# A list scheduler's table: measured durations, and one port shared by GpSimd and VectorE

## The chip, the cores and the metric

The kernel runs on one core of one Trainium2 chip. The metric is the device time of one execution in microseconds (us), the median of several runs. A core has five instruction streams that run side by side and meet only at semaphores: PE (TensorE, matrix products), DVE (VectorE), ACT (ScalarE), POOL (GpSimd) and SP (SyncE, which here issues nearly all DMA transfers). Each stream runs in program order: an instruction that waits holds up all that stands behind it on its engine.

## The reference

One decoder block over 16 meta tokens and 1024 tokens of width 1024, in float32. It has a differential-attention branch (a) and a gated-linear-attention branch (b, GLA below), whose gated sum goes through a last projection and a norm.

```
u = rms_norm(h, norm_w);  proj = u @ w_in          (1040 x 1024 @ 1024 x 9232)
a_q, a_k, a_v, a_z, g_q, g_k, g_v, g_z, g_lr, gate_a, gate_b = split(proj)
(branch a: 8 heads, partial rope on q and k, two causal softmaxes per head)
p = softmax(q1 k1) - lam * softmax(q2 k2)
y_a = (rms_norm(p @ v) * silu(a_z)) @ w_branch_a
(branch b: 4 heads of width 128, values of width 256)
b = cumsum(log_sigmoid(g_lr @ gate_w2 + gate_b) / 16)
a[t, j] = sum_c q[t, c] k[j, c] exp(b[t, c] - b[j, c])   for j <= t
o = a @ v + (q exp(b)) @ state;  state = exp(b_last) state + (k exp(b_last - b))' v
y_b = (rms_norm(o) * silu(g_z)) @ w_branch_b
out = rms_norm(h + (sigmoid(gate_a) y_a + sigmoid(gate_b) y_b) @ w_out)[16:]
```

## The kernel before, in words

Products in float32 are made of three products of halves (high x high, high x low, low x high), so that most groups of PE instructions come in threes. The program has four parts, one behind the other.

1. The first norm, the transposes of x and the four g_k projections (0 to 79.8 us).
2. Most of the input projections, as Strassen products in a fixed order (79.8 to 594 us).
3. The GLA stage (594 to 891 us): four heads, each in two halves of 512 tokens. Among the work of the heads lie *fillers*: projections that later stages need (`Jobs.cols` L410 to L412 and `Jobs.rows` L431 to L438, results in tiles `ps_proj`), with `rope(0, ...)` for the attention's rotated queries.
4. Attention over eight heads, with the projection of branch b between, then that of branch a, then the output projection and the last norm (891 to 1399 us).

Parts 1, 3 and 4 are not written in program order. Each operation is entered in a list (`Schedule.op`) with its engine, an estimated duration, what it depends on, the buffer ring from which it takes a slot and a priority. `Schedule.run` then plays the list through once, when the program is built: it keeps a time for each engine, starts the operation that can start earliest, and within 0.05 us of a tie the one with the better priority. Each engine's program order is the order of these planned starts; the durations in the list have no other effect. Part 2 does not pass through it.

A half of a GLA head goes through seven *levels* (L1437 to L1482): POOL makes four differences of the cumulated decay (L1398, tile `xl`), ACT takes their exponential (L1441), DVE multiplies them by k and q (L1405), PE makes the *level product* (L1412, tile `ps_l`), and DVE picks the part of it that counts (L1416). There are two buffers each for `xl` and `ps_l`. Behind the levels come the diagonal (L1422), the output (L1488, L1489), the state (L1476, L1482), a norm (L1504), the transposes (L1509) and the split and store of the result (L1514 to L1525). POOL does the last step of that split (L1521) and SP stores it to `d_ob`.

When the last GLA operation and its store are done, a step in SP's list (`change`) closes the stage's buffers. Attention takes their place: POOL clears the tiles `vm` (L1593), and the loads of values and later keys follow (`early`).

Of the kernel before, what the change touches and what calls it, by code (L numbers as in the profile page):

```python
# [67 lines left out]

class Schedule:
# [9 lines left out]
    def op(self, eng, us, run, deps=(), take="", use=(), prio=0.0, lat=None):  # L79
        o = Op(eng=eng, us=us, run=run, deps=deps, take=take, use=use, prio=prio)  # L80
# [10 lines left out]
    def run(self):  # L91
        now = dict.fromkeys(("PE", "ACT", "DVE", "POOL", "SP"), 0.0)
        ready = {e: [] for e in now}
# [27 lines left out]
        while len(order) < len(self.ops):  # L121
            best = None
            for e in now:
                pick = None
                for o in ready[e]:
                    r = at(o)
                    if r is not None:
                        r = max(r, now[e])
                        if pick is None or r < pick[0] - AHEAD:
                            pick = (r, o)  # L130
# [4 lines left out]
            now[o.eng] = o.end  # L135
            if o.take:
# [12 lines left out]
def tile_hybrid_block(  # L149
# [191 lines left out]
    class Jobs:  # L341
# [7 lines left out]
        def weights(self, src, us_lo=0.6, eng="DVE", scale=None, where=None, ring="w", pre=None):  # L349
# [31 lines left out]
            for c in range(2):  # L381
                a = op("ACT", 0.52, lambda c=c: hi(c), (ld,) + tuple(w["ops"]), take="" if c else ring,
                       use=(("raw", ld),), prio=PR["W"])
                b = op(eng, us_lo, lambda c=c: lo(c), (a,), use=(("raw", ld),), prio=PR["W"])
# [14 lines left out]
        def cols(self, ws, pieces, evac):  # L399
            prev = None  # L400
            for t0, n in pieces:
                for i, w in enumerate(ws):
                    b = {}

                    def run(kc, b=b, w=w, t0=t0, n=n):
# [9 lines left out]
                        [lambda k=k, run=run: run(k) for k in range(KC)], n / 512 * 0.64,  # L415
# [4 lines left out]
        def rows(self, src, evac, pre=None):  # L420
# [221 lines left out]
    with ExitStack() as es:  # L642
# [15 lines left out]
        def x_tile(i):  # L658
# [28 lines left out]
            r = op("POOL", 0.3, root, (m,), prio=-1)  # L687
            d = op("DVE", SCU, scale, (r,), use=(("xt", ld),), prio=-1)
# [167 lines left out]
        W = [jobs.weights(c[0], 1.2, "POOL") if i < 2 else jobs.weights(c[0]) for i, c in enumerate(cols)]  # L856
# [18 lines left out]
        def sums(k):  # L875
            ts, x = {}, {}
            for i in range(1, 5):
# [16 lines left out]
                t = ts[i] = op("DVE", 0.6, run, (R[r], R["t", 1, k]) + tuple(readers.get(r, ())), prio=30 + k,  # L894
# [4 lines left out]
            for i in range(1, 5):  # L899
# [13 lines left out]
                b = op("DVE", 0.6, lo, (a,) + free("l") + last.get((i, 1), ()), prio=30 + k, use=use)  # L913
# [142 lines left out]
    with ExitStack() as es:  # L1056
# [110 lines left out]
        def rope(base, dst, pieces, lo_t, pre=(None, None)):  # L1167
# [18 lines left out]
            def turns(a, t0, n):  # L1186
# [8 lines left out]
                for q, f in ((0, ALU.subtract), (1, ALU.add)):  # L1195
# [12 lines left out]
                    for s in range(3):  # L1208
                        prev = (op("DVE", n / 960 + 0.07, lambda s=s, turn=turn: turn(s), prev,
# [29 lines left out]
        def gla_head(h):  # L1239
# [10 lines left out]
            for t0, n in KP:  # L1250
# [11 lines left out]
                def low(v=v, c=c, first=t0 == 0):  # L1262
# [11 lines left out]
                    g("DVE", 0.43, lambda v=v, c=c: tt(d["lg"][:, c], d["lg"][:, c], v["t"], ALU.subtract), (m, l),  # L1274
# [4 lines left out]
            for i, (t0, n) in enumerate([(0, NM)] + [(NM + P * i, P) for i in range(8)]):  # L1279
# [3 lines left out]
                if i == 0 or i % 2:  # L1283
# [4 lines left out]
                    scans.append(g("DVE", 0.2, scan, deps, use=(lgu,)))  # L1288
                else:
# [9 lines left out]
                    s = g("DVE", 0.2, scan, deps, take="scn", use=(lgu,))  # L1299
                    scans.append(g("DVE", 0.26, rest, (s,), use=(("scn", s), lgu)))  # L1300
# [32 lines left out]
            def half_ops(hf, st):  # L1333
# [1191 lines left out]
```

## Time and profile before

| | us |
|---|---|
| median of 3 runs | 1395.36 (1394.68 to 1396.65) |
| the profiled execution, its own time | 1400.65 |
| its span, first to last instruction | 1398.9 |
| mean granted TensorE clock | 0.990 |

The trace is of one execution, 5.3 us longer than the median of the runs; 1.75 us of it lie outside the span. Times in the text are from the start of that span. The names of tiles are the program's, with the line that issued the instruction.

### The profile page before, as it was taken

Reading aid. Unit: us, or ns where it says so; the run is one execution under the profiler, and the core shown is the slowest. Engines: PE = TensorE matmul, PEld = TensorE weight load, DVE = VectorE, ACT = ScalarE, POOL = GpSimd, SP = SyncE. Lnnn points to the kernel's source line nnn. Section 1 sums busy time; section 2 is a strip of 40 time slices with the busy share of each in tenths; the row PEclk is TensorE's granted clock in tenths of the full one; section 3 lists DMA queues with packets and bytes.
Section 4 is the critical chain, followed back from the end, with each engine's and each line's share of the span. In section 5 each row is a group of like instructions: output and inputs, shape, how many; then the busy total and the mean of one; then the engine's idle time right before and its main releaser. Section 6 shows DMA issues by size and latency. Waiting matters only on the chain.

```text
span 1398.9 us, 22432 instructions
## 1 busy us (share of the span) xinstructions
PE 1337.4 (96%) x7736; PEld 1158.8 (83%) x7736; DVE 908.3 (65%) x1613; ACT 741.1 (53%) x1608; POOL 626.1 (45%) x731
## 2 busy tenths in 40 slices
PE   6999999999999999988998989999999999999998
PEld 6988889899888888787888979878888888887786
DVE  4745463545555444478888887568777777657775
ACT  7543232653665666554544544568677777522343
POOL 3112232442544233236566475347576665535434
PEclk9999999999999999999999999999999999999999
DMA  6216473324333323385531465769765564678332
GB/s 222 90 67 200 141 231 122 106 84 145 113 113 114 120 99 105 116 287 150 178 119 64 150 205 167 246 201 292 275 224 171 194 208 140 241 271 278 109 119 84
DMA packets 126337, 229.50 MB, mean 164 GB/s; under 512 B 13568, under 2 KB 51648, under 8 KB 126224
## 3 DMA queue, kind: packets, MB, share of 16 engines
q1 hardware_dynamic: 125936, 227.03, 49.2%
q8 instruction: 61, 1.00, 0.3%
q0 software_dynamic: 288, 1.05, 0.3%
q14 instruction: 52, 0.43, 0.1%
HBM read 143.81 MB, written 84.21 MB: 163 GB/s over the span
## 4 chain that ended last, share of the span: by engine, by line
PE 67%; DVE 13%; DMA 5%; issue 5%; POOL 5%; ACT 4%; SPq 1%; POOLq 0%; DVEq 0%; ACTq 0%
PE ps_st L547 28%; PE ps_st L572 6%; DVE xl L1405 3%; PE ps_t L2321 2%; PE ps_s L1698 2%; PE ps_proj L410 2%; PE ps_proj L412 2%; PE ps_proj L411 2%; PE ps_l L1412 2%; PE ps_s L1699 1%; PE ps_y L2321 1%; PE ps_s L2321 1%; PE ps_t L1812 1%; PE ps_y L1981 1%; PE ps_y L1983 1%
## 5 line engine op out<-in xcount | busy, mean ns | idle before, releaser
L495 POOL TENSOR_TENSOR s<-w_raw 128x512 f32<-128x512 f32 x48 | 70.2, 1481 | 199.5 <-DMA w_raw<-in_w_col_dram 146.4
L547 PE MATMUL ps_st<-th,wh 128*128 128x512 f32 x352 | 137.3, 390 | 0.2 <-DVE u L561 0.2
L547 PE MATMUL ps_st<-tl,wh 128*128 128x512 f32 x352 | 137.1, 389 | 0.0
L547 PE MATMUL ps_st<-th,wl 128*128 128x512 f32 x352 | 136.9, 389 | 0.0
L1398 POOL TENSOR_TENSOR xl<-lg 128x128 f32<-128x128 f32 x224 | 108.8, 513 | 60.1 <-PE ps_l L1412 21.2
L230 DVE TENSOR_TENSOR wl<-s,wh 128x512 fp32r<-128x512 f32 x96 | 76.1, 792 | 63.6 <-ACT wh L229 63.5
L229 ACT CAST wh<-s 128x512 fp32r<-128x512 f32 x96 | 59.3, 618 | 105.6 <-PE ps_st L547 51.5
L1727 DVE TENSOR_REDUCE nm<-ps_s 128x1 f32<-128x272 f32 (+7 forms) x128 | 96.5, 765 | 18.9 <-PE ps_s L1701 18.0
L410 PE MATMUL ps_proj<-u_hi,w_hi 128*128 128x346 f32 (+3 forms) x320 | 105.1, 329 | 3.2 <-DVE cc L561 1.7
L1739 ACT ACTIVATE p<-ps_s,nm 128x272 f32<-128x272 f32 (+7 forms) x128 | 96.5, 756 | 19.2 <-DVE nm L1727 13.3
L547 PE MATMUL ps_st<-u_hi,wh 128*128 128x512 f32 x264 | 104.2, 395 | 1.0 <-issue 1.0
L547 PE MATMUL ps_st<-u_lo,wh 128*128 128x512 f32 x264 | 105.0, 398 | 0.0
L547 PE MATMUL ps_st<-u_hi,wl 128*128 128x512 f32 x264 | 103.8, 393 | 0.0
L411 PE MATMUL ps_proj<-u_lo,w_hi 128*128 128x346 f32 (+3 forms) x320 | 99.0, 309 | 0.1
L412 PE MATMUL ps_proj<-u_hi,w_lo 128*128 128x346 f32 (+3 forms) x320 | 98.3, 307 | 0.0
L229 ACT CAST wh<-w_raw 128x512 fp32r<-128x512 f32 x70 | 43.2, 617 | 95.4 <-PE ps_st L547 87.8
L230 DVE TENSOR_TENSOR wl<-w_raw,wh 128x512 fp32r<-128x512 f32 x70 | 59.8, 854 | 49.7 <-ACT wh L229 49.7
L1751 POOL TENSOR_SCALAR p<-p,r,nlam 128x144 f32<-128x144 f32 (+3 forms) x64 | 56.4, 882 | 56.2 <-DVE r L1747 42.8
L495 POOL TENSOR_TENSOR s<-w_raw,s 128x512 f32<-128x512 f32 x22 | 28.4, 1293 | 114.1 <-DVE wl L230 114.1
L547 PEld LDWEIGHTS ps_st<-th,wh 128*128 128x128 f32 x352 | 66.1, 188 | 14.8 <-ACT sg L273 0.6
L547 PEld LDWEIGHTS ps_st<-th,wl 128*128 128x128 f32 x352 | 66.1, 188 | 14.0
L547 PEld LDWEIGHTS ps_st<-tl,wh 128*128 128x128 f32 x352 | 66.1, 188 | 13.8
(402 smaller groups left out, 4390.2 us busy)
## 6 DMA issues: line engine op xcount, KB each, us to landing
w_raw<-in_w_col_dram SPq DMA_DIRECT2D x54, 512.0 KB, 3.6
q<-d_q SPq DMA_DIRECT2D x32, 512.0 KB, 5.1
kk<-d_k SPq DMA_DIRECT2D x16, 520.0 KB, 6.0
d_g<-sg SPq DMA_DIRECT2D x32, 256.0 KB, 2.0
va<-d_v SPq DMA_DIRECT2D x16, 512.0 KB, 5.2
d_q<-qhi SPq DMA_DIRECT2D x24, 256.0 KB, 3.1
d_q<-qlo SPq DMA_DIRECT2D x24, 256.0 KB, 3.6
w_raw<-in_w_row_dram SPq DMA_DIRECT2D x12, 512.0 KB, 3.6
```

Source lines behind the costliest of these rows:

```text
L229: nc.scalar.copy(hi, raw)
L230: (eng or nc.vector).tensor_tensor(lo, raw, hi.bitcast(F32), ALU.subtract)
L410: mm(b["ps"], wh, rh, start=kc == 0, stop=False)
L411: mm(b["ps"], wh, rl, start=False, stop=False)
L412: mm(b["ps"], wl, rh, start=False, stop=kc == KC - 1)
L495: nc.gpsimd.tensor_tensor(r, x, y, op)
L547: mm(ps, w[:, k], x[k], start=start and k == 0 and i == 0, stop=k == KC // 2 - 1 and i == 2, skip_group_check=not start,)
L572: mm(ps[ti // 2][:, r], x[k][:, c], w[:, k % 2], start=start and k == i == 0 and ti % 2 == 0, stop=k == KC // 2 - 1 and i == 2 and ti % 2 ...
L1398: nc.gpsimd.tensor_tensor(dst, x if e else ref, ref if e else x, ALU.subtract)
L1727: nc.vector.tensor_reduce(b, ps, AX.XY if len(ps.shape) == 3 else AX.X, ALU.max, negate=True)
L1739: act(dst, ps, AF.Exp, bias=b, accum_out=stat[t]["sm"][:, j : j + 1])
L1751: nc.gpsimd.tensor_scalar(p2, p2, stat[t]["r"][:, 1:2], nlam, ALU.mult, ALU.mult)
```

## The change

Two things in the list change, and no operation is added or removed: each engine has as many instructions as before. First, durations: the three-part PE products are entered as `mm3(n)`, 3 x (n/2400 + 0.0135) us (0.68 for 512 columns, where 0.64 stood; 0.36 for 256, where 0.33 stood), and POOL's operations are mostly longer (1.2, 1.13 and 1.23 become 1.28; 0.36 becomes 0.40; the last weight 2.3 becomes 3.2). Second, a port: all POOL operations but the small roots (`POOL-`), and those DVE operations that are now entered as `DVE+`, may not overlap in the plan. The multiplications L1405 and the DVE operations that read PSUM stay plain `DVE`. What the program does with the buffers and the semaphores is as before. Line numbers behind the new functions are 15 higher in the changed kernel (L1412 becomes L1427, L436 becomes L451).

```diff
+def plus(eng):
+    return "DVE+" if eng == "DVE" else eng
+
+def mm3(n):
+    return 3 * (n / 2400 + 0.0135)
...
     def op(self, eng, us, run, deps=(), take="", use=(), prio=0.0, lat=None):
-        o = Op(eng=eng, us=us, run=run, deps=deps, take=take, use=use, prio=prio)
+        port = eng in ("POOL", "DVE+")
+        eng = eng.strip("+-")
+        o = Op(eng=eng, us=us, run=run, deps=deps, take=take, use=use, prio=prio, port=port)
...
     def run(self):
         now = dict.fromkeys(("PE", "ACT", "DVE", "POOL", "SP"), 0.0)
+        port = 0.0
...
-                        r = max(r, now[e])
+                        r = max(r, now[e], port if o.port else 0.0)
...
             now[o.eng] = o.end
+            if o.port:
+                port = o.end
...
-                        [lambda k=k, run=run: run(k) for k in range(KC)], n / 512 * 0.64,
+                        [lambda k=k, run=run: run(k) for k in range(KC)], mm3(n),
...
-                            [lambda k=k, ti=ti: run(ti, k) for k in kh], 0.33 if ti else 0.22,
+                            [lambda k=k, ti=ti: run(ti, k) for k in kh], mm3(256) if ti else 0.24,
...
-                        prev = (op("DVE", n / 960 + 0.07, lambda s=s, turn=turn: turn(s), prev,
+                        prev = (op("DVE+", n / 960 + 0.07, lambda s=s, turn=turn: turn(s), prev,
...
-                        prev = (g("POOL", 0.36, lambda i=i: diff(li, i), sc + prev, take="" if i else "xl", use=(lgu,)),)
+                        prev = (g("POOL", 0.4, lambda i=i: diff(li, i), sc + prev, take="" if i else "xl", use=(lgu,)),)
                         if i == 0:
                             own = ("xl", prev[0])
                     e = g("ACT", 0.52, lambda: act(X["xl", li], X["xl", li], AF.Exp, scale=1.0 / 16), prev)
                     s = []
                     for i in range(4):
                         u, o = (gq[hf], d["qop"][hf]) if i % 2 else (gk, d["kop"])
                         s.append(g("DVE", 0.2, lambda i=i: scale_(li, i), (e, o), use=(u,)))
...
-                kd = g("DVE", 0.6, lambda: tt(X["kd"], X["kd"], kh(), ALU.mult), (kd, d["kop"]), use=(gk,))
-                qe = g("DVE", 0.6, qef, (eb, d["qop"][hf]), take="qe", use=(gq[hf],))
+                kd = g("DVE+", 0.6, lambda: tt(X["kd"], X["kd"], kh(), ALU.mult), (kd, d["kop"]), use=(gk,))
+                qe = g("DVE+", 0.6, qef, (eb, d["qop"][hf]), take="qe", use=(gq[hf],))
...
-            s = op("POOL", nk * 1.2e-3 + 0.1, lambda: second(t), (r,), prio=b)
-            FB_[t] = op("DVE", nk / 960 + 0.07, lambda: both(t), (s,),
+            s = op("POOL", nk * 0.84e-3 + 0.34, lambda: second(t), (r,), prio=b)
+            FB_[t] = op("DVE+", nk / 960 + 0.07, lambda: both(t), (s,),
...
-        fl = op("POOL", 2.3, lambda: nc.gpsimd.tensor_scalar(tiles["fw"], tiles["fw"], float(D) ** 0.5, None, ALU.mult), (fl,), prio=2000)
+        fl = op("POOL", 3.2, lambda: nc.gpsimd.tensor_scalar(tiles["fw"], tiles["fw"], float(D) ** 0.5, None, ALU.mult), (fl,), prio=2000)
```

Three places of the new order follow. The first is PE in the GLA stage at the first levels of the last head, head 3. Before, from its third level product (L1412) on: filler products (L436 to L438) stand between it and the next step, the state (L1476), and so it goes on to the end of the head.

```order
L1412 MATMUL ps_l<-xl 128x128 x2
L436 MATMUL ps_proj<-w_hi,u_hi 128x256
L437 MATMUL ps_proj<-w_hi,u_lo 128x256
L438 MATMUL ps_proj<-w_lo,u_hi 128x256
L1476 MATMUL ps_d<-gv,kt 128x256
```

With the change, from the second level product of head 3 (L1427) on: L451 to L453 are filler, L1491 the state, L1437 the diagonal.

```order
L1427 MATMUL ps_l<-xl 128x128 x2
L451 MATMUL ps_proj<-w_hi,u_hi 128x256
L452 MATMUL ps_proj<-w_hi,u_lo 128x256
L453 MATMUL ps_proj<-w_lo,u_hi 128x256
L1491 MATMUL ps_d<-gv,kt 128x256
L1427 MATMUL ps_l<-xl 128x128 x10
L1437 MATMUL ps_l<-gq,gk 128x128 x4
L1427 MATMUL ps_l<-xl 128x128 x2
```

What moved is the filler: the three products L451 to L453 in this piece are the last of it, but for 16 short ones of the meta rows at the stage's end. Behind them five level products (two matmuls each) stand in one row, where before fillers stood between them.

The second place is PE at the end of the stage. Before, around the last transposes of head 3 (L1509):

```order
L437 MATMUL ps_proj<-w_hi,u_lo 128x256
L438 MATMUL ps_proj<-w_lo,u_hi 128x256
L1509 MATMUL ps_t<-ident,oc 128x128 x4
L436 MATMUL ps_proj<-w_hi,u_hi 128x256
L437 MATMUL ps_proj<-w_hi,u_lo 128x256
```

Behind this, 109 more filler products and 16 short ones of the meta rows (L431, L432) stood ahead of the first attention scores (L1698). With the change, around the last outputs (L1503, L1504) and the last transposes (L1524):

```order
L1503 MATMUL ps_o<-st,qe 128x256
L1504 MATMUL ps_o<-gv,at 128x256
L1524 MATMUL ps_t<-ident,oc 128x128 x8
L446 MATMUL ps_y<-w_hi,um 48x256
L447 MATMUL ps_y<-w_lo,um 48x256
```

The filler behind the last transposes is gone from this place: only the short products of the meta rows (L446, L447, 16 in all) stand between them and the scores.

The third place is DVE in the last two heads, at the rope of the attention's queries (L1203: products with the loaded tile `rr`). Before, they stood in head 3, in the middle of the four multiplications (L1405) of a level:

```order
L1405 TENSOR_TENSOR xl<-xl,gk 128x32x4
L1405 TENSOR_TENSOR xl<-xl,gq 128x32x4
L1405 TENSOR_TENSOR xl<-xl,gk 128x32x4
L1203 TENSOR_TENSOR qks<-rr,cs 128x512 x4
L1205 TENSOR_TENSOR qks<-qks 128x512 x2
L1405 TENSOR_TENSOR xl<-xl,gq 128x32x4
L1416 COPY_PREDICATED mx_5662<-masks,ps_l 128x256
L1143 SCALAR_TENSOR_TENSOR qks<-qks 128x512 x2
```

With the change the same work (L1218, L1220, L1158) stands in the first half of head 2, and one by one between the level's multiplications (L1420):

```order
L1472 TENSOR_TENSOR kd<-kd,gk 128x512
L1431 COPY_PREDICATED mx_5662<-masks,ps_l 128x256
L1218 TENSOR_TENSOR qks<-rr,cs 128x512
L1420 TENSOR_TENSOR xl<-xl,gk 128x16x8
L1218 TENSOR_TENSOR qks<-rr,cs 128x512
L1220 TENSOR_TENSOR qks<-qks 128x512
L1218 TENSOR_TENSOR qks<-rr,cs 128x512
```

The block of four products has moved one head forward and is spread out. In parts 1 and 4 the operations move too, by less: on PE in part 4 by at most 21 places. On PE the order of all that follows the last attention product is unchanged.

## Rows read from the trace of the kernel before

**Rows 1.** The page, section 1, with busy time and share of the span.
```profile
PE 1337.4 (96%) x7736; PEld 1158.8 (83%) x7736; DVE 908.3 (65%) x1613; ACT 741.1 (53%) x1608; POOL 626.1 (45%) x731
```

**Rows 2.** Windows of four stretches, busy time, then clock, DMA share, GB/s.
```profile
79.80:594.00 514.20, 512.27 (x2585) 434.35 (x2585) 255.42 (x344) 255.78 (x430) 175.33 (x130) 1.00 0.39 127
594.00:891.00 297.00, 270.37 (x1808) 252.33 (x1809) 232.64 (x572) 140.05 (x339) 163.62 (x284) 0.98 0.53 167
891.00:1215.00 324.00, 315.04 (x2057) 267.42 (x2056) 249.12 (x437) 234.41 (x621) 193.98 (x230) 0.99 0.65 216
1215.00:1399.00 184.00, 172.64 (x771) 140.64 (x769) 121.32 (x162) 60.67 (x120) 77.37 (x62) 0.97 0.53 181
```

**Rows 3.** Waits of PE, with us in total, times, longest.
```profile
PE ps_l L1412 <- DVE xl L1405: 15.2, 21, 2.6
```

**Rows 4.** Two lines, with ns of shortest, median, longest, first and last start.
```profile
L1405 DVE TENSOR_TENSOR xl<-xl,gq x112: 270/284/1366, 623.7 to 860.1; 128x128 f32<-128x128 f32 x112
L1398 POOL TENSOR_TENSOR xl<-lg x224: 391/445/3246, 612.6 to 855.0; 128x128 f32<-128x128 f32 x112
```

**Rows 5.** Groups of DVE and POOL, 594 to 891, busy us, mean ns.
```profile
L1504 DVE TENSOR_SCALAR oc<-oc,ro 128x256 f32<-128x256 f32 x32 | 12.0, 426 | 5.3 <-POOL ro L1542 5.3
L1457 DVE TENSOR_TENSOR kd<-kd,gk 128x512 f32<-128x512 f32 x8 | 6.4, 801 | 1.6 <-ACT kd L1456 1.5
L1521 POOL TENSOR_TENSOR ob<-ob,oh 128x512 fp32r<-128x512 f32 x16 | 25.1, 1567 | 25.3 <-ACT oh L1518 23.1 <-issue 1.3 <-POOL xl L1398 0.9
L1428 POOL TENSOR_TENSOR at<-mx,tri 128x256 f32<-128x256 f32 x16 | 11.8, 749 | 18.9 <-DVE mx L1416 18.8
L1364 POOL TENSOR_TENSOR kd<-lg 128x256 f32<-128x256 f32 x16 | 10.9, 687 | 0.6 <-DVE lg L1297 0.6
```

**Rows 6.** Windows of two parts of that stretch, all lines.
```profile
594.00:822.80 228.80, 205.68 (x1321) 190.29 (x1321) 190.31 (x462) 114.98 (x275) 132.45 (x230) 0.99 0.51 161
822.80:874.80 52.00, 49.41 (x361) 46.96 (x362) 38.08 (x103) 21.24 (x56) 27.78 (x49) 0.97 0.56 180
```

**Rows 7.** Windows of the same parts, tile ps_proj alone, the filler projections.
```profile
594.00:822.80 228.80, 150.14 (x860) 130.05 (x860) 9.95 (x20) 15.31 (x36) 0.99 0.51 161
822.80:874.80 52.00, 33.58 (x229) 29.89 (x230) 1.66 (x4) 3.69 (x10) 0.97 0.56 180
874.80:890.90 16.10, 13.38 (x111) 13.19 (x111) 2.12 (x5) 1.86 (x5) 1.00 0.71 216
```

**Rows 8.** Timeline of PE near 823 us, with start and length.
```profile
822.79 0.71 PE L1412 MATMUL ps_l<-xl 128*128 128x128 f32 x4 [2.55 <-DVE xl L1405]
823.46 0.28 PE L437 MATMUL ps_proj<-w_hi,u_lo 128*128 128x256 f32 x1
823.58 0.28 PE L438 MATMUL ps_proj<-w_lo,u_hi 128*128 128x256 f32 x1
```

**Rows 9.** Timeline of PE, the second level product of head 1.
```profile
694.92 0.38 PE L1412 MATMUL ps_l<-xl 128*128 128x128 f32 x1 [0.39 <-DVE xl L1405]
```

**Rows 10.** The transposes L1509 of head 1 and of head 3.
```profile
L1509 PE MATMUL ps_t<-ident,oc x16: 270/272/327, 720.5 to 740.8; 128*128 128x128 f32 x16
L1509 PE MATMUL ps_t<-ident,oc x16: 271/273/328, 853.2 to 874.8; 128*128 128x128 f32 x16
```

**Rows 11.** Timeline of POOL and of PE behind head 3.
```profile
884.67 0.34 POOL L1593 MEMSET vm<- 80x128 f32 x2 [2.70 <-DMA d_ob<-ob]
901.04 0.28 PE L1833 MATMUL ps_v<-pm,vm 80*128 80x256 f32 x1
```

**Rows 12.** DMA issues from 880 to 902, KB each, median us to landing.
```profile
vm<-d_v SPq DMA_DIRECT2D x6, 8.0 KB, 5.4
```

**Rows 13.** Windows of two stretches near 637 us.
```profile
634.10:637.50 3.40, 1.22 (x9) 1.09 (x10) 3.40 (x13) 0.63 (x1) 2.02 (x5) 1.00 0.80 191
637.50:640.90 3.40, 3.40 (x14) 3.21 (x13) 3.04 (x9) 1.72 (x3) 2.38 (x6) 0.50 0.66 227
```

**Rows 14.** Timeline of DVE near 830 us.
```profile
829.97 2.50 DVE L1203 TENSOR_TENSOR qks<-rr,cs 128x512 f32<-128x512 f32 x4 [1.73 <-DMA rr<-d_rq]
```

More of the change, by code (lines that the diff above doesn't have):

```diff
@@ L686, in x_tile @@
             m = op("DVE", 0.07, mean, (s,), prio=-1)
-            r = op("POOL", 0.3, root, (m,), prio=-1)
-            d = op("DVE", SCU, scale, (r,), use=(("xt", ld),), prio=-1)
+            r = op("POOL-", 0.55, root, (m,), prio=-1)
+            d = op("DVE+", SCU, scale, (r,), use=(("xt", ld),), prio=-1)
             return v, ("xt", ld), d
@@ L855, in tile_hybrid_block @@
         cols += [] if GQ else [(w_col[19], d_gq[3], NM, 128 ** -0.5, QP)]
-        W = [jobs.weights(c[0], 1.2, "POOL") if i < 2 else jobs.weights(c[0]) for i, c in enumerate(cols)]
+        W = [jobs.weights(c[0], 1.28, "POOL") if i < 2 else jobs.weights(c[0]) for i, c in enumerate(cols)]
         def job(i, pieces):
@@ L892, in run @@
                     raws[r] = dst
-                t = ts[i] = op("DVE", 0.6, run, (R[r], R["t", 1, k]) + tuple(readers.get(r, ())), prio=30 + k,
+                t = ts[i] = op("DVE+", 0.6, run, (R[r], R["t", 1, k]) + tuple(readers.get(r, ())), prio=30 + k,
                                take="xt" if k == 3 and i == 3 else "", use=xuse(("t", 1, k)) + ((("xt", ts[3]),) if k == 3 and i == 4 else ()))
@@ L912, in sums @@
                 a = op("ACT", 0.48, hi, (ts[i],) + free("h") + last.get((i, 0), ()), prio=30 + k, use=use)
-                b = op("DVE", 0.6, lo, (a,) + free("l") + last.get((i, 1), ()), prio=30 + k, use=use)
+                b = op("DVE+", 0.6, lo, (a,) + free("l") + last.get((i, 1), ()), prio=30 + k, use=use)
                 last[i, 0], last[i, 1] = (a,), (b,)
@@ L1541, in half_ops @@
                 r = g("DVE", 0.08, rstd_in, tuple(ocs))
-                r = g("POOL", 0.96, lambda: nc.gpsimd.tensor_tensor(X["ro"], X["ro"], mhalf[:, :4], ALU.pow), (r,))
-                nr = tuple(g("DVE", 0.26, lambda n=n: norm(n), (r,)) for n in range(4))
+                r = g("POOL-", 1.0, lambda: nc.gpsimd.tensor_tensor(X["ro"], X["ro"], mhalf[:, :4], ALU.pow), (r,))
+                nr = tuple(g("DVE+", 0.26, lambda n=n: norm(n), (r,)) for n in range(4))
                 for vh in range(2):
@@ L1927, in value @@
                 first = b == 0
-                last = op("PE", 0.67 + 0.11 * first, lambda b=b: apply_v(n, b),
+                last = op("PE", 0.71 + 0.12 * first, lambda b=b: apply_v(n, b),
                           (tl, v) + ((ml, vm) if first else (last,)) + ((A_[n - 1],) if first and n else ()),
@@ L2041, in tile_hybrid_block @@
         for i in range(0, KC, 2):
-            ws = [jobs.weights(w_bb[i + j], 1.2, "POOL") for j in range(2)]
+            ws = [jobs.weights(w_bb[i + j], 1.28, "POOL") for j in range(2)]
             for j, c in ((0, 0), (1, 0), (0, 1), (1, 1)) if i == 0 else ((0, 0), (0, 1), (1, 0), (1, 1)):
@@ L2205, in term @@
                 d = (ops[x1],) if isinstance(x1, str) else ()
-                ops[name] = op(CB[name], 0.62 if CB[name] == "DVE" else 1.13, run, tuple(lds) + (tuple(ops.values()) or prev_ld) + (s4op,), take="x4",
+                ops[name] = op(plus(CB[name]), 0.62 if CB[name] == "DVE" else 1.28, run, tuple(lds) + (tuple(ops.values()) or prev_ld) + (s4op,), take="x4",
                                use=use + tuple(("x4", x) for x in d), prio=BP[0])
@@ L2401, in norm @@
                     if pre:
-                        d += (op("POOL", 1.13, times, (res[i][c * (n - 2)], fl), use=(ring(i, c),), prio=pr),)
-                    a = op("ACT" if pre else "DVE", 0.62, scale, d, use=(ring(i, c),), prio=-1 if not final else i)
+                        d += (op("POOL", 1.28, times, (res[i][c * (n - 2)], fl), use=(ring(i, c),), prio=pr),)
+                    a = op("ACT" if pre else "DVE+", 0.62, scale, d, use=(ring(i, c),), prio=-1 if not final else i)
                     op("SP", 0.75, store, (a,), use=(ring(i, c),), prio=-1)
```

56 lines of the change are left out of this document (28 added, 28 removed).

## The prediction

> **What bounds the kernel now.** I read the page's busy times first: PE is busy for 96% of the span, and no other engine comes near [rows 1]. So a new order can only win or lose time in which PE waits. Then the busy times by stretch: in the Strassen part, which the list doesn't order, PE is busy for 512.27 of 514.20 us; in the GLA stage for 270.37 of 297.00, in the attention for 315.04 of 324.00 and in the tail behind it for 172.64 of 184.00 [rows 2]. The three ordered stretches hold 26.6, 9.0 and 11.4 us of idle PE. The GLA stage has the most, and it is also where the order changes most: on PE 167 of 576 operations stand out of their old sequence.
>
> Who is waited for there? In the list of waits the largest of PE is the level product L1412 behind the multiplications L1405 on DVE: 15.2 us in 21 waits [rows 3]. Those multiplications, and the differences on POOL that feed them, stretch: L1405 has a median of 284 ns and a longest of 1366, L1398 one of 445 and up to 3246 [rows 4]. DVE and POOL are busy for 232.64 and 163.62 us of the same 297.00 [rows 2], together 396, so they lie beside each other for 99 us at least.
>
> **The change part by part.** No instruction is added or removed, so all of the effect is order. Four moves matter.
>
> *Filler goes forward in the GLA stage.* Before, when the second level product of head 3 starts at 822.79 [rows 8], 229 + 111 = 340 of the stage's 1200 filler matmuls are still to come [rows 7]. In the new order all but three of them stand ahead of that point (first order piece). In a run without waits they start 0.12 us apart, 823.46 to 823.58 [rows 8]; 0.117 over a longer run; so 40 us of PE work move from behind this product to ahead of it.
>
> What does this do to the product's time? Before, it starts 228.8 us into the stage. I added the spacings, in unhindered runs, of the 1321 matmuls ahead of it [rows 6] and get 191 us; 38 us are lost to waits, restarts at half clock and gaps too short for the busy time (which counts a matmul to its modelled end, so it reads 205.68 [rows 6]). With 40 to 41 us more ahead of it the product can't start before 191 + 41 = 232, and if nothing of the loss were covered it would start at 270. Most of it is covered: in the new order PE's own work puts the first product of head 2 at 169 us into the stage, 12 us later than it was measured, and that of head 3 at 228, 4 later, so from head 2 on the heads' chains run ahead of PE. In heads 0 and 1 PE's work and the measured chain come within 3 us of each other, and there waits of a few us stay. I allow 3 us at the start of the stage, 6 in heads 0 and 1 and nothing behind: 241.
>
> *Head 3 runs bare.* From its second product to its last transposes PE then has only the head's own work. Before, this stretch took 822.79 to 874.8, 52 us [rows 8, 10], with 229 filler matmuls in it [rows 7], so it was never short of work: PE was busy for 49.41 of 52.00 [rows 6]. How long is it without? The nearest row is head 1: second product at 694.92, last transposes at 740.8 [rows 9, 10], 45.9 us, with filler between. The lower end is that PE held this chain up at half of its steps, by one filler job of about 1 us each at some 12 steps before and behind it: 40. The upper end is that of head 3, 52. I take 45: the chain goes through POOL, ACT, DVE and PE in turn, and only PE's step gets free. So the last transposes start at 241 + 45 = 286 us into the stage, at 880 on the old scale, where they stood at 874.8 [rows 10]: **+5.2 us**.
>
> *Nothing covers the hand-over.* Before, behind the last transposes 111 filler matmuls covered 13.38 us [rows 7], while the last result was split and stored, `vm` cleared (POOL L1593 at 884.67, released by the store) and loaded (5.4 us a load [rows 12]); the first product with values came at 901.04 [rows 11], 26.2 us behind the last transposes. The steps of this hand-over are a chain of SP, POOL and DMA that doesn't get shorter, but for about 1 us by which PE and not the load came last: **-1.2 us**. So the old cover of 13.4 us turns into idle PE; that is no further loss, since the same filler was done earlier, but PE waits there for several us, and behind such a wait the granted clock halves: near 637 us, behind a stretch with PE busy for 1.22 of 3.40 us, it reads 0.50 for 3.40 us [rows 13]. That costs half of 3.4 where PE is full: **+1.7 us**.
>
> *The rope moves out of head 3.* Before, DVE stood still for `rr` in the middle of a level and then did 2.5 us of L1203 in one piece [rows 14], which PE felt as about 4 us. In the new order that work lies in head 2, where PE has filler. This is in the 241 and the 45 and isn't counted again.
>
> *Attention, tail and first part.* On PE the first 10 us of the attention are in the old order; then scores come up to 7 us earlier and the projection of branch b later, by at most 21 places. The idle time of 9.0 us and the slow starts [rows 2] are all that can be won; longer POOL entries (the second softmax product) make the list start the softmax steps earlier. Bounds: all of the 9.0 won, or 4 lost by one more long wait like the 2.55 us of [rows 8]. I take **-2 us**. In the tail behind the attention PE's order is the same, and DVE's differs by single places: within 1 us. In the first part ACT does one more weight cast ahead of the first transposed tile, 0.6 us late at the start: 0 within 0.7.
>
> Sum: 5.2 - 1.2 + 1.7 - 2 = +3.7 us. Against the profiled execution's 1400.65 this is 1404.4; that execution lies 5.3 above the median of the runs, 1395.36, so the forecast is 1399.1.
>
> **The rule for the port.** The rows show a stretch, not a stop: POOL's L1398 has a median of 445 ns for a least time of 391, and DVE's multiplications a median near the least [rows 4], though both engines are busy for most of the stage. The Trainium skill ("SBUF — State Buffer", "Who interferes with whom") says that VectorE and GpSimd share a pair of ports under an exclusive lock, so that the loser stops. For the bare tail of head 3 this gives a sum of its own: 48 differences at 391 ns, 48 multiplications at 270 [rows 4], four L1521, four L1428, two L1364, eight L1504 and one L1457 at their means [rows 5] are 18.8 + 13.0 + 6.3 + 3.0 + 1.4 + 3.4 + 0.8 = 46.7 us one behind the other, with no gap for ACT or PE. If the lock held all through, a tail of 50 to 52 would follow in place of 45, as rival 3 has it, and also a planner that is right about the hardware. Against the full rule: the 99 us at least in which both engines are busy.
>
> **The rivals.**
> 1. *Faster: the filler ahead buys out the waits, and the bare tail is short.* The waits of head 0 and 1 are covered as well (product at 236) and the tail takes 41: last transposes at 277, 4 us earlier than before. With 1.2 from the hand-over, 1.7 lost at half clock and 5 won in the attention: -3.8 - 1.2 + 1.7 - 5 = -8.3, 1387. For it: the 15.2 us of waits for L1405 [rows 3] and all of [rows 14] sit where filler now stands ahead. Against: the filler is the same total, and 11 to 13 us of cover behind the last transposes are given up. It decides if the product at 241 comes before 237.
> 2. *No change:* the product at 240, a tail of 43, the attention as in the forecast: last transposes at 283, +2.2 - 1.2 + 1.7 - 2 = +0.7, 1396.
> 3. *Slower by more:* the ports hold the tail at 51, so the last transposes come at 292, +11.2 - 1.2 + 1.7 = +11.7; the attention wins nothing: 1407.
> 4. *The change does nothing,* since the queues wait for each other in the same places: can't be, with 167 operations moved; it would look like rival 2.
>
> **How the numbers follow.** The forecast (+3.7, own range +2.8 to +8) gets 0.29, rival 3 0.17, rivals 2 and 4 0.23, rival 1 0.31. A difference below 0.2% (2.8 us) is about what a measurement of this kernel can't tell from none. Faster 0.31, same 0.23, slower 0.46. The range leaves out a tenth at each side: from 1386, just past rival 1, to 1409, past rival 3.
>
> **What would show it.** In the changed profile no instruction on `ps_proj` lies behind the third level product of head 3; the second one starts at 833 to 837 (241 right; at 830 rival 1, at 842 more waits stayed); PE is busy for less than half of the 45 us behind it; the last transposes start at 879 to 882; POOL clears `vm` 10 us later, and the first product with values starts at 904 to 907, with PE idle for most of the 10 us ahead of the scores and a clock of 0.5 behind. Wrong would be: last transposes before 875, or an attention stretch (first product with values to 1215) more than 7 us shorter, or longer than before.

## The result and the profile after

The changed kernel takes 1439.15 us (median of 4 runs, 1435.18 to 1440.91) against 1396.01 for the kernel before (4 runs): 43 us more, ratio 1.0296 with a 95% interval of 1.0268 to 1.0324. The forecast was 1399.1 with a range to 1409. "Slower" had the largest chance, 0.46, and came; the size was far off.

One statement ahead of the prediction is wrong, and it matters below: the text and the excerpt of the diff there have the level multiplications L1405 as plain `DVE` in the changed list. The change marks them too:

```diff
-                        s.append(g("DVE", 0.2, lambda i=i: scale_(li, i), (e, o), use=(u,)))
+                        s.append(g("DVE+", 0.2, lambda i=i: scale_(li, i), (e, o), use=(u,)))
```

So in the plan no multiplication of a level may lie beside a difference on POOL.

The profiled execution of the changed kernel has 1435.18 us, 34.5 above that of before. First the page's busy times, then those by stretch, cut at the places of the program where [rows 2] cuts, to within 1 us (Strassen part, GLA stage to the first attention scores, to the last value product of the attention, end).

```profile
PE 1351.1 (94%) x7736; PEld 1167.2 (81%) x7736; DVE 905.7 (63%) x1613; ACT 739.3 (52%) x1608; POOL 607.3 (42%) x731
```

```profile
82.50:596.60 514.10, 512.09 (x2585) 434.31 (x2585) 257.17 (x344) 255.74 (x430) 175.31 (x130) 1.00 0.38 127
596.60:927.10 330.50, 285.19 (x1808) 261.18 (x1809) 234.50 (x572) 138.51 (x337) 149.03 (x280) 0.93 0.47 149
927.10:1254.10 327.00, 316.40 (x2063) 268.82 (x2062) 244.02 (x438) 234.38 (x622) 189.19 (x234) 0.99 0.65 213
1254.10:1433.40 179.30, 169.41 (x765) 137.31 (x763) 118.33 (x160) 59.81 (x119) 77.48 (x62) 0.99 0.55 191
```

The Strassen part is as long as before. The GLA stage is 330.5 us, where it was 297.0, and PE is idle in it for 45.3 us in place of 26.6, at a clock of 0.93 in place of 0.98. The same 1808 matmuls keep PE busy for 285.2 us where it was 270.4. Of the two stretches behind it the first is 3.0 us longer and the second 4.7 shorter. Now PE in head 3: the second level product, some that follow, and the last two groups of transposes (start, length, instruction, the idle time before it and who ended it).

```profile
867.87 0.68 PE L1427 MATMUL ps_l<-xl 128*128 128x128 f32 x4 [0.16 <-DVE xl L1420]
...
873.32 0.68 PE L1427 MATMUL ps_l<-xl 128*128 128x128 f32 x4 [2.10 <-DVE xl L1420]
876.05 2.05 PE L1427 MATMUL ps_l<-xl 128*128 128x128 f32 x8 [2.05 <-DVE xl L1420]
880.58 1.20 PE L1427 MATMUL ps_l<-xl 128*128 128x128 f32 x4 [2.48 <-ACT xl L1456]
...
919.56 1.26 PE L1524 MATMUL ps_t<-ident,oc 128*128 128x128 f32 x4 [3.15 <-DVE oc L1519]
921.67 1.12 PE L1524 MATMUL ps_t<-ident,oc 128*128 128x128 f32 x4 [0.84 <-DVE ob L1529]
```

The second product starts 271.3 us into the stage (596.6 to 867.87; before 228.8), the last transposes at 921.67, 53.8 us later. Before it was 51.7, counted in the same way up to this row:

```profile
874.47 0.60 PE L1509 MATMUL ps_t<-ident,oc 128*128 128x128 f32 x4
```

Between the two PE waits at most steps, for 0.3 to 3.2 us; it is busy for 32 of 54 us. In that stretch the clock is at 0.72, and in two other stretches of the stage with long waits it falls too, one at the start of head 0, one in head 2 (columns as in [rows 13]):

```profile
868.00:922.00 54.00, 32.08 (x129) 23.56 (x130) 31.54 (x86) 14.86 (x41) 24.25 (x49) 0.72 0.16 49
```

```profile
620.00:625.00 5.00, 1.75 (x12) 1.47 (x10) 3.99 (x11) 1.82 (x5) 1.24 (x3) 1.00 0.85 289
625.00:630.00 5.00, 4.13 (x12) 3.11 (x13) 5.00 (x10) 1.79 (x5) 5.00 (x8) 0.51 0.51 152
```

```profile
800.00:810.00 10.00, 6.04 (x46) 5.37 (x45) 7.66 (x21) 2.42 (x4) 4.51 (x12) 0.97 0.91 285
810.00:820.00 10.00, 7.63 (x36) 6.41 (x36) 6.40 (x15) 4.04 (x14) 5.95 (x14) 0.86 0.47 164
```

The first product with values waits for its load and comes 19.7 us behind the last transposes (before 26.6):

```profile
941.37 0.36 PE L1848 MATMUL ps_v<-pm,vm 80*128 80x256 f32 x1 [2.78 <-DMA vm<-d_v]
```

The ledger of the two profiled executions: +2.6 us at the start of the GLA stage, +42.5 to head 3's second product, +2.1 from there to the last transposes, -6.9 to the first product with values, -5.8 from there to the end, in sum +34.5.

DVE shows something that the prediction didn't look at. Its picks (L1416, now L1431), which wait for PE's level product, cost it before:

```profile
DVE mx L1416 <- PE ps_l L1412: 6.5, 14, 1.3
```

and with the change:

```profile
DVE mx L1431 <- PE ps_l L1427: 26.2, 34, 2.2
```

### The profile page after: what moved, and what is told of

Read it like the earlier page. It is cut to its first block, busy times and chain, and to the rows that moved or that the text cites. A ratio compares the mean times of both kernels' runs of the same rounds, so it can differ in the third digit from the quotient of the medians.

```text
span 1433.4 us, 22439 instructions
## 1 busy us (share of the span) xinstructions
PE 1351.1 (94%) x7736; PEld 1167.2 (81%) x7736; DVE 905.7 (63%) x1613; ACT 739.3 (52%) x1608; POOL 607.3 (42%) x731
## 5 line engine op out<-in xcount | busy, mean ns | idle before, releaser
L1413 POOL TENSOR_TENSOR xl<-lg 128x128 f32<-128x128 f32 x224 | 98.3, 466 | 86.0 <-PE ps_l L1427 38.9
L1713 PE MATMUL ps_s<-kk,q 128*128 128x264 f32 (+7 forms) x208 | 74.8, 363 | 0.3
```

Source lines behind the costliest of these rows:

```text
L1413: nc.gpsimd.tensor_tensor(dst, x if e else ref, ref if e else x, ALU.subtract)
L1713: mm(pp, qh, kk[:, c0 : c0 + w], start=True, stop=False)
```

## The experiments

Each kernel was timed against the kernel before on the same chip; its ratio's 95% interval stands in brackets. A switch by list was built into the changed kernel; the first five runs are settings of it, and with both sets empty it has the order of before, with both full that of the change.

```diff
+PORT, DUR = (0, 1, 2), (0, 1, 2)    # first part, GLA stage, attention and tail
+def either(old, new):
+    return new if Schedule.stage in DUR else old
...
-        port = eng in ("POOL", "DVE+")
+        port = Schedule.stage in PORT and eng in ("POOL", "DVE+")
...
-            [lambda k=k, run=run: run(k) for k in range(KC)], mm3(n),
+            [lambda k=k, run=run: run(k) for k in range(KC)], either(n / 512 * 0.64, mm3(n)),
```

**Durations alone** (`PORT, DUR = (), (0, 1, 2)`).

> New durations in all three lists, no port. Theory (the port in the plan lets the list use up the filler early, so that the last GLA head runs bare): the fillers keep their places by head as in the kernel before (122 us of them ahead of head 3's second product, 125 before), so the last transposes start near 875 to 880 us and the time is 1390 to 1402. Rival (the new durations of the fillers and of POOL's work are what moves the order): 1425 to 1445.

1420.2 us, ratio 1.018 [1.0148, 1.0213]: neither. The filler does keep its place (348 matmuls of 256 columns are left behind head 3's second product, 324 before), and still 24 us are lost. **Port alone** (`(0, 1, 2), ()`).

> The port in all three lists, durations of before. Theory: as the changed kernel, 1430 to 1445, with no filler behind head 3's second product and its last transposes at 915 to 925 us. Rival: near the kernel before, 1390 to 1405.

1424.5, 1.0214 [1.0184, 1.0244]: 6 us below the theory's range, with the last transposes at 916.4 and no filler behind the second product, as it had them. The two parts alone add up to 53 us, more than the 43 of both together. **Both in the GLA list alone** (`(1,), (1,)`).

> Both parts of the change in the list of the GLA stage alone, the other two lists as before. Theory: all of the loss sits there and the attention's new order gives some 6 us back, so this is slower than the changed kernel: 1440 to 1450, first product with values at 938 to 944 us. Rival (a good part of the loss lies in the attention or in the first part): below 1425.

1436.2, 1.0292 [1.0261, 1.0324]: 40 of the 43 us sit in that list. The theory had it slower than the changed kernel, and it isn't: the attention's new order gives nothing back. **Both in the list of the attention and tail alone** (`(2,), (2,)`).

> Both parts of the change in the list of the attention and the tail alone, the other two as before. Theory: the gain that the attention shows in the changed kernel is its own: 1386 to 1393, faster than before by 3 to 9 us. Rival (that gain is only work done while the start was late): 1394 to 1400.

1395.2, 1.0003 [0.9988, 1.0019]: no change, as the rival had it. **The port there alone** (`(2,), ()`).

> The port in the list of the attention and the tail alone, durations of before everywhere. Theory (of what the attention won it was the port that won it, the new durations gave some back): 1385 to 1392, with 486 to 491 us from the first product with values to the end. Rival (as with both parts in that list, a gain of a few us that later starts take back): 1392 to 1399.

1390.9, 0.9967 [0.9951, 0.9983]: faster than before by 0.33%, in the theory's range. The products with values show where each loss lies: in this row of a line its first and last start are the start of the attention's value products and their end. Changed kernel, durations alone, port alone, both in the attention, port in the attention:

```profile
L1848 PE MATMUL ps_v<-pm,vm x32: 280/364/387, 941.4 to 1254.1; 80*128 80x256 f32 x32
```

```profile
L1857 PE MATMUL ps_v<-pm,vm x32: 281/364/388, 912.2 to 1236.7; 80*128 80x256 f32 x32
```

```profile
L1857 PE MATMUL ps_v<-pm,vm x32: 280/364/552, 935.9 to 1244.0; 80*128 80x256 f32 x32
```

```profile
L1857 PE MATMUL ps_v<-pm,vm x32: 280/364/386, 904.3 to 1214.7; 80*128 80x256 f32 x32
```

```profile
L1857 PE MATMUL ps_v<-pm,vm x32: 281/364/373, 904.4 to 1209.7; 80*128 80x256 f32 x32
```

Before, it is 315.0 us:

```profile
L1833 PE MATMUL ps_v<-pm,vm x32: 279/364/387, 901.0 to 1216.0; 80*128 80x256 f32 x32
```

The GLA stage thus ends 11 us later with the durations, 35 with the port, 40 with both. In the attention the durations alone cost 9.5 us (324.5), the port alone wins 9.7 (305.3) and both win 4.6 (310.4). These are single executions, and the one of before is 5 us over its median; by the medians of the runs the port alone wins 4.8 and both 0.6. Durations and port are not two steps of one improvement: in the attention one spoils part of what the other wins.

**Early filler, without the change.** In the kernel before, the GLA list is kept from planning head 3's products until all but two filler steps are planned.

```diff
+        held = sum(o.eng == "PE" and o.prio >= 1000 for o in self.ops) - 2 if Schedule.stage == 1 else 0
...
+                    if held > 0 and e == "PE" and 315 < o.prio < 400:
+                        continue
```

> The kernel before (no port, old durations) with one rule more in the list of the GLA stage: head 3's products may not be planned until all filler but two steps is. So 40 us of filler stand ahead of head 3, as in the changed kernel, and nothing else of the change is there. Theory: the last transposes start at 900 to 912 us, and the time is 1415 to 1430. Rival (filler ahead costs nothing by itself): 1393 to 1402.

1425.5, 1.023 [1.021, 1.025]. Early filler alone costs 30 us; its first product with values is at 931.6. The second product of head 3 starts at 865.49, as late as in the changed kernel, but the bare tail behind it, to the last transposes at 911.29, takes only 45.8 us (the second row, columns as in [rows 13]). The run holds head 3 back until the filler is done, so it can't show whether filler spread over the heads would be covered.

```profile
L1862 PE MATMUL ps_v<-pm,vm x32: 279/364/553, 931.6 to 1243.5; 80*128 80x256 f32 x32
865.50:911.30 45.80, 28.99 (x139) 22.70 (x137) 32.11 (x84) 15.34 (x41) 27.57 (x54) 0.84 0.18 58
```

**Filler rationed by head** (`due`: up to the first product of heads 1, 2, 3 no more filler than before).

```diff
+        fill, due = 0.0, {115.75: 57.3, 215.75: 87.1, 315.75: 123.7} if Schedule.stage == 1 else {}
...
+                    if due and e == "PE" and o.prio >= 1000 and fill + o.us > min(due.values()):
+                        continue
```

> The changed kernel, with one rule more in the list of the GLA stage: up to the first level product of heads 1, 2 and 3 no more filler may be planned than the kernel before has there (57.3, 87.1 and 123.7 us). Durations, port and all else stay. Theory (the loss is the filler that head 3 and the hand-over behind it lack): the last transposes start at 872 to 885 us and the time is 1392 to 1405. Rival (the order in which the port puts the work of DVE and POOL within a head is what costs): above 1415.

1441.4, 1.0335 [1.0318, 1.0352]: the time of the rival, yet the run doesn't decide for it, since in this order a head's ration was used up before the head's end, and each step from one head to the next then ran bare, as ahead of head 3, where no filler runs from 845.1 to 868.6:

```profile
850.00:860.00 10.00, 3.19 (x8) 1.48 (x8) 9.07 (x19) 3.13 (x7) 4.02 (x6) 0.50 0.86 289
```

**PE's order and the other engines' orders, crossed.** A list of operation numbers fixes PE's order in the GLA stage to that of before, and the rest is planned as changed; then the reverse.

```diff
+PE_ORDER = [...]
...
+                    if seq and e == "PE" and o.n != seq[0]:
+                        continue
```

> The changed kernel, with PE's order in the GLA stage fixed to that of the kernel before; the list still plans DVE, ACT, POOL and SP with the port and the new durations, there and elsewhere. Theory (the place of the filler in PE's order is the loss, and rationing it by head only moved the bare stretches to the ends of the heads): last transposes at 873 to 885 us, 1390 to 1405. Rival (the order within DVE and POOL that the port makes costs by itself): above 1415.

> The kernel before, with PE's order in the GLA stage fixed to that of the changed kernel; all else is planned without the port and with the old durations. Theory: nearly all of the loss appears, last transposes at 912 to 925 us, 1425 to 1440. Rival: 1395 to 1410.

1444.6, 1.0345 [1.0318, 1.0372], and 1444.9, 1.0345 [1.0322, 1.0369]. Each half alone brings more than the whole loss. With PE's old order PE waits for the multiplications nearly three times as long as in [rows 3]:

```profile
PE ps_l L1444 <- DVE xl L1437: 40.9, 23, 7.6
```

So early filler isn't all of it, and the two can't simply be added. The order of DVE shows one reason: of the 48 picks that have a next level in their half, 37 stood behind multiplications of that level before, 14 with the change. Where a pick stands ahead and DVE waits for PE, the multiplications behind the pick wait with it, ready or not.

**The pick behind the next level's multiplications,** a dependency in the list of the changed kernel, and the same with PE's old order.

```diff
-                    pre = product(li, *lv, pre)
+                    pre = product(li, *lv, pre + tuple(nxt[0] if nxt else ()))
```

> The changed kernel with one dependency more in the list: the pick of a level comes behind the multiplications of the next level, so that all 48 picks have them ahead. The filler stays as early as in the changed kernel (166 us ahead of head 3's second product). Theory: the lead of a level is back and only the loss of the early filler is left, as in the run that moved filler in the kernel before: 1415 to 1430. Rival (the lead is of no account): 1434 to 1445.

> The changed kernel with both put back: PE's order in the GLA stage fixed to that of the kernel before, and the pick of a level behind the next level's multiplications. Theory (early filler and lost lead are all of it): 1393 to 1408, against 1444.6 for PE's order alone. Rival (a third thing in the orders of ACT, POOL and DVE): above 1420.

1427.7, 1.0225 [1.0201, 1.0249], and 1442.2, 1.0326 [1.0304, 1.0347]. The first is as expected: DVE's waits at the pick fall to 5.5 us, 11.5 us come back, and what is left is about the price of early filler. The second fails: PE still waits 43.0 us for multiplications, so something else in the other engines' orders holds the chain. What it is wasn't isolated; its timeline has places like the last rows here, where the four multiplications of a level are split by operations that wait for others (`qe`, `ro`).

```profile
DVE mx L1440 <- PE ps_l L1436: 5.5, 8, 1.0
```

```profile
L1857 PE MATMUL ps_v<-pm,vm x32: 280/364/550, 933.2 to 1245.8; 80*128 80x256 f32 x32
```

```profile
665.83 0.69 DVE L1387 TENSOR_TENSOR qe<-gq,eb 128x512 f32<-128x512 f32 x1 [1.55 <-PE ps_o L1520]
666.47 0.29 DVE L1437 TENSOR_TENSOR xl<-xl,gk 128x128 f32<-128x128 f32 x1
666.68 0.29 DVE L1437 TENSOR_TENSOR xl<-xl,gq 128x128 f32<-128x128 f32 x1
667.74 0.17 DVE L1533 TENSOR_SCALAR ro<-sso 128x4 f32<-128x4 f32 x1 [0.78 <-ACT sqo L1530]
667.82 0.29 DVE L1437 TENSOR_TENSOR xl<-xl,gk 128x128 f32<-128x128 f32 x1
```

**The mark taken off the multiplications** in the changed kernel, and the same with PE's old order.

```diff
-                        s.append(g("DVE+", 0.2, lambda i=i: scale_(li, i), (e, o), use=(u,)))
+                        s.append(g("DVE", 0.2, lambda i=i: scale_(li, i), (e, o), use=(u,)))
```

> The changed kernel with one mark taken back: the multiplications of the GLA levels are entered as DVE again, not DVE+. In the order, 30 of 48 picks then have the next level's multiplications ahead of them (37 in the kernel before, 14 in the changed one), and 150 us of filler stand ahead of head 3's second product (125 before, 166 changed). Theory (two losses: filler taken early, and DVE's lead of a level lost since the port forbids a multiplication beside a difference): about half of the loss goes, 1408 to 1425. Rival (the loss is the port on other operations, or the durations): above 1430.

> The changed kernel with PE's order in the GLA stage fixed to that of the kernel before and the level multiplications unmarked (DVE, not DVE+). It differs from the run with PE's order alone fixed (1444.6) by the mark only. Theory (the mark spoils DVE's order by itself: multiplications that are ready stand behind operations that wait): 1396 to 1412. Rival (any plan made around another plan's order of PE loses by the mixture): above 1425.

1406.2, 1.0065 [1.0044, 1.0086], better than expected: without this one mark 33 of the 43 us are gone. The waits at the pick are near the old ones, and 129 filler matmuls of 256 columns lie between head 3's second product and the scores (3 in the changed kernel, 324 before):

```profile
DVE mx L1440 <- PE ps_l L1436: 9.5, 15, 2.4
```

```profile
L1857 PE MATMUL ps_v<-pm,vm x32: 280/364/386, 911.2 to 1223.8; 80*128 80x256 f32 x32
```

With PE's old order the mark's removal wins 20 us (1424.8, 1.0225 [1.0204, 1.0246]), and 30 stay: between the two expectations. So with PE's order held the mark costs 20 us through the other engines' orders. The 30 may be what planning around another plan's PE order costs; no run parts that from the other marks and the durations.

**The mark alone** in the kernel before: port in the GLA list for POOL and the multiplications only, no new durations.

> The kernel before, with the port in the list of the GLA stage alone, and there for POOL's operations and the level multiplications alone; no other DVE operation is marked and no duration is changed. In the order 15 to 19 of 48 picks have multiplications of the next level ahead of them, and 154 us of filler stand ahead of head 3's second product. Theory (this one mark is most of the loss): 1418 to 1434. Rival (the mark costs only together with the new durations and the other marks): 1396 to 1410.

1403.9, 1.0069 [1.0053, 1.0086]: the rival. The mark is dear only in company. Here 102 filler matmuls were left for head 3, and its first product with values is at 909.1:

```profile
L1857 PE MATMUL ps_v<-pm,vm x32: 279/364/386, 909.1 to 1219.7; 80*128 80x256 f32 x32
```

**Extra matmuls in head 3's bare part,** to keep the clock up (here the lighter form; the heavier has 512 columns, and 5 to 14 matmuls at a step where this one has 2 or 3).

```diff
+                    if hf or li > 2:
+                        idle(3)
...
+                def idle(n):
+                    if h == GH - 1:
+                        t = jobs.bank()
+                        for _ in range(n):
+                            mm(t[:, :256], u_hi[:, 0, :P], u_hi[:, 0, :256], start=True, stop=True)
```

> The changed kernel with extra matmuls on PE in the bare part of head 3, into a bank that nothing reads (7 of 512 columns behind each level product from the fourth on, 7 behind each group of transposes, 14 behind the last output of a half, 5 behind a state product of the second half). They do no work for the result and only keep PE busy. Theory (8 of the 54 us of the bare tail are steps of PE at half clock): the clock stays at 1.00 there, the tail from the second product to the last transposes falls to 44 to 48 us, and the time is 6 to 12 us under the changed kernel. Rival (the tail is the latency of the chain through POOL, ACT and DVE alone): 52 to 56 us, and the time is the changed kernel's or worse.

> As the run with extra matmuls in the bare part of head 3, but a fifth to a half of them: 3 of 256 columns behind a level product or a group of transposes, 2 behind a state product and behind the last output of a half. In the heavier run they kept the clock up but held PE for 1.5 us at each step, so it said nothing on the clock. Theory (8 of the 54 us are half clock): the tail falls to 45 to 50 us where the clock stays at 1.00, and the time is 4 to 9 us under the changed kernel. Rival (latency of the chain alone): 52 to 56 us and no gain.

1443.7, 1.0347 [1.0325, 1.0369], and 1437.6, 1.0293 [1.027, 1.0316]. The heavy form held the clock (two stretches of the bare part in the first rows) but PE with it, and its tail took 60.0 us. The light one lifted it only in part, from 0.72 to 0.85; its tail took 51.5 us, and the time moved by 1.5 us, inside the spread. What half clock costs there stays open.

```profile
890.00:902.00 12.00, 12.00 (x60) 9.95 (x59) 5.95 (x21) 3.99 (x15) 4.74 (x11) 1.00 0.01 1
902.00:914.00 12.00, 11.32 (x58) 9.21 (x57) 6.09 (x16) 3.29 (x6) 5.19 (x9) 1.00 0.36 131
```

```profile
871.00:925.00 54.00, 36.57 (x189) 30.34 (x188) 32.59 (x88) 15.18 (x42) 25.49 (x51) 0.85 0.17 54
```

**Port in the attention, and the pick behind the multiplications,** for a faster kernel.

> The port in the list of the attention and the tail alone, durations of before, and in the GLA stage the pick behind the next level's multiplications (48 of 48 have them ahead, 37 in the kernel before). Theory: the waits of level products for multiplications (15.2 us in the kernel before) fall to 5 to 10 and the time is 1380 to 1389, below the 1390.9 without that dependency. Rival (the filler covered those waits anyway, or the later pick costs as much): 1388 to 1396.

1394.0, 0.9988 [0.9973, 1.0002]: the rival; the dependency wins nothing where the lead is there anyway. The fastest kernel of the study is the port in the attention's list alone.

## Why the prediction was wrong

**What bounds the kernel: right.** PE and the GLA stage decided; the Strassen part didn't move, and the run with the change in the GLA list alone has nearly all of it.

**"Most of it is covered ... 241": this step failed,** by 30 us (271). The floor of 232 and the end without any cover, 270, were right; the choice between them was not. The argument was that from head 2 on the chains ran ahead of PE, since PE's work put the products later than they had been measured. But the measured times belonged to the old order of all engines. By the spacing count, an estimate, 39 us were lost ahead of the second product, about as much as the 38 of before. Heads 0 and 1 lost 14 us where they had lost 20 (the prediction allowed 6); by a second count of that kind the gain lies inside their first halves, and the three steps from one head to the next lost as much as before, with or without filler. The start of head 0 lost 6 more (PE busy for 1.75 of 5 us from 620, then clock 0.51), and head 2 some 3 more, where the prediction allowed nothing.

Why so little was covered is known in part. DVE's picks, which wait 26.2 us where they waited 6.5, are the smaller part: with these waits at 5.5 us the second product still starts at 864.4, 3.5 us sooner. Without the mark on the multiplications it starts at 844.2; of these 24 us some 15 are the 126 filler matmuls that this order leaves for later (at 0.117 us), and some 9 are fewer losses. The rest stays open. The prediction traced the moves on PE, took DVE's order as given but for the rope, and misread the mark on the multiplications.

**"I take 45" for the bare tail: too short** by 9 us for this order, but not for the move of the filler as such: with early filler alone the tail is 45.8, and with PE's new order and the old plan for the others 46.3. The other 8 us come from the order of the other engines, about 5 of them from the picks (49.1 us where their place is mended, row below). The tail full of filler was 51.7. So 213 filler matmuls between the steps of a chain, some 25 us of PE's time, had cost it about 6 us, and taking them out wins back no more than that: 40 us of PE work, most of which rode along in head 3, had to be paid in full ahead of it. That is the core of the loss, and the run with early filler alone prices it at 30 us; the place of the picks adds 11.5, and the two together are near the 43. The amount left counts: 324 matmuls left (before), first product with values at 901; 129 and 102 left, 911 and 909; 6 or fewer, 932 to 941 (951 with PE's new order alone). These orders differ in more than the filler, and more isn't better: with the durations alone 348 are left and it comes at 912.

```profile
864.40:913.50 49.10, 31.80 (x125) 24.06 (x125) 28.71 (x84) 13.13 (x37) 25.28 (x48) 0.74 0.11 38
```

**-1.2 and +1.7 at the hand-over: mis-sized.** It took 6.9 us less than before. The prediction held that its chain doesn't get shorter; it did. POOL cleared `vm` 7.1 us behind the start of the last transposes (before 10.2), and the loads were issued 4.5 us behind that (before 7.8, with three rows of stores of filler results in SP's stream between, now one). The first load took 1.4 us more (7.6), and PE came 0.5 us behind its landing where it had come 2.4 behind, last by 2 us and not by 1. The issue of the loads before, then clearing and issue with the change:

```profile
892.47 3.75 SPq L1615 DMA_DIRECT2D vm<-d_v  x6
```

```profile
928.78 0.34 POOL L1608 MEMSET vm<- 80x128 f32 x2 [2.38 <-DMA d_ob<-ob]
933.29 5.15 SPq L1630 DMA_DIRECT2D vm<-d_v  x6
```

Half clock cost more than one stretch of 3.4 us: the mean clock of the stage fell from 0.98 to 0.93. How much of the 54 us is half clock wasn't settled.

**-2 for attention and tail:** -5.8 in the profiled executions, in the range given. It isn't the new list's merit alone: with the old list behind the same late start (GLA list alone) the value products took 311.5 us, 3.5 less than before.

**The rule for the port.** "A stretch, not a stop" was read from medians. The difference of 3246 ns [rows 4] is a stop: it starts 0.02 us behind the first of a row of DVE instructions that follow each other without a gap, near their least times, and ends 0.26 us behind the last of them (POOL's difference, then the first and the last of that row):

```profile
626.04 3.25 POOL L1398 TENSOR_TENSOR xl<-lg 128x128 f32<-128x128 f32 x1 [3.94 <-PE ps_l L1412]
626.02 0.69 DVE L377 TENSOR_TENSOR w_lo<-w_raw,w_hi 128x512 fp32r<-128x512 f32 x1
628.34 0.69 DVE L1355 TENSOR_TENSOR qe<-gq,eb 128x512 f32<-128x512 f32 x1
```

The Trainium skill ("SBUF — State Buffer", "Who interferes with whom") speaks of an exclusive lock. This row agrees with it; that the lock held all through the tail isn't shown, since the 46.7 us that the prediction added up for that case are no floor: the tail with early filler alone took 45.8. POOL reads as busy while it is stopped, so the 99 us in which both engines are busy say little against the lock either. The tail of 53.8, near the 50 to 52 of rival 3, came about through order.

With the change the longest difference is 928 ns (1513 with the durations alone, 1600 with the port alone),

```profile
L1413 POOL TENSOR_TENSOR xl<-lg x224: 390/442/928, 616.0 to 901.0; 128x128 f32<-128x128 f32 x112
```

and all of them take 98.3 us of busy time where they took 108.8. So the long collisions are gone, and the kernel is slower. PE's waits for the multiplications didn't fall:

```profile
PE ps_l L1427 <- DVE xl L1420: 17.9, 18, 2.1
```

**Rivals and range.** Rival 3 had the right side and the wrong cause. The range ended at 1409, just past rival 3. The prediction's own two upper ends, 270 for the product and 52 for the tail, together put the last transposes 41 us later than before, near the measured loss, but they were never carried into the range.

## What to carry to other kernels

A list scheduler's resource model acts through order alone: a resource made exclusive in the plan doesn't just part collisions. Here it made a chain look longer in the plan, and what fills gaps was then spent early. Check on every engine which ready instructions come to stand behind one that waits, and how much filler is left for the last chain, before pricing the move on the bounding engine. Where a cost has two ends worked out from the trace, carry both through to the sum.

## What was not expected of the hardware

A chain of small steps through four engines took 51.7 us with 213 filler matmuls of 256 columns between its steps, and 45.8 to 55.7 us without them, by the order of the other engines. One difference on POOL, 0.39 us at the least, took 3.25 us beside a row of DVE instructions without a gap. With the change such collisions are shorter (10 us less of busy time on POOL's differences), and the kernel is slower all the same.
